# Tying every weight split behind the evacuation of the last item

## The chip, the cores and the metric

The kernel runs on one core of a Trainium2 chip. The metric is the device time of one execution in microseconds (us). An engine is named by its short form: PE is TensorE, DVE is VectorE, ACT is ScalarE, POOL is GpSimd, SP is SyncE, which here issues loads. Each engine works through its own list of instructions in order, and an instruction whose inputs are not ready holds up all that stand behind it on that engine.

## The reference

One layer of a decoder trunk on a sequence of 512 tokens of width 1024. Three causal mixers are fed from one projection, merged by gates, and followed by a squared-ReLU MLP with a gated per-layer embedding:

```python
proj = x @ w_in
(da_q, da_k, da_v, sb_q, sb_k, sb_v, dl_q, dl_k, dl_v, gates) = jnp.split(proj, ...)
o_da = diff_attention(da_q, da_k, da_v, lam, da_norm, ...)   # 4 heads, two softmax maps each
o_sb = stick_breaking_attention(sb_q, sb_k, sb_v)            # 8 heads
o_dl = dilated_attention(dl_q, dl_k, dl_v, ...)              # 3 groups x 4 heads
g = jax.nn.sigmoid(gates)
merged = g0 * (o_da @ w_branch_da) + g1 * (o_sb @ w_branch_sb) + g2 * (o_dl @ w_branch_dil)
x = layer_norm(ALPHA * x + merged @ w_out)
hid = jax.nn.relu(x @ w_up)
c = jnp.square(hid) @ w_down
ple = jax.nn.sigmoid(x @ w_ple_gate) * (p @ w_ple)
x = layer_norm(ALPHA * x + c + ple)
```

## The kernel before

**Items and splits.** All large products are cut into items (the list `items`). An item is a run of matmuls into one bank of PSUM (`mm`), with the function that copies or adds the finished bank out (`ev`, the evacuation). Weights come in blocks of 128 x 1024. SP loads a block into one of five `raw` buffers, or POOL and SP first sum two blocks (`total`). Each block is then split in two parts that the matmuls need: ACT rounds `raw` to `wh` (L255), and DVE subtracts, `wl = raw - wh` (L258). Each product then takes three matmuls: high by high, high by low, low by high (L84 to L86, for example). `wh` and `wl` live in a ring of seven buffers, so a split can run only when PE has read the block of seven splits ago for the last time; a `raw` buffer comes free when the `wl` made from it is done.

**The loop.** For each item n the loop at the end of the kernel (L1607) makes sure that the blocks that the item needs are split, evacuates the item before it (L1617), issues one to three further splits ahead of need (`pump`, L1619), lets one step of the attention heads run beside it, and writes the item's matmuls. Plain items use two banks in turn, so an evacuation has the time of one item before PE needs the bank again; a product that an attention head reads has no such time.

**Order.** The kernel is written through a scheduling layer that may move an instruction ahead of others on its engine by priority. `tc.issue_after(i)` gives one order that it must keep: what is issued inside stands behind `i` on the same engine. It adds no semaphore. `issue_split` (L233) issues each split behind the instructions in the list `tie`. Only the first stick-breaking head fills that list (L1309), and it is emptied at n = 8 (L1621); from there on splits are not tied to anything but their buffers and data.

**Stages.** In the order of time, with the places that the prediction speaks of:

- to about 470 us: the projections, with the heads between them. A dilated head makes two rows of logits L0 and L12 (L1450, L1466, from `dl_k` and `dl_q`; `dl_k` is evacuated at L322), a normaliser over its three groups (L1484 to L1513, with two small matmuls L1491 and L1493), scales its rows (L1515, L1519), transposes them (L1531, L1540; copies `pt0`, `pt12`), and multiplies with `dl_v` (L1552, L1557). A differential head evacuates `da_k` (L122 to L129), makes logits (L135, L136), a softmax difference `lg` (L1394) and transposes it (L1399).
- 470 to 690 us: gates, branches and `w_out`. Gate products are made by a recursive scheme with cut copies (`cut`, L460 to L477).
- 690 to 735 us: the gates of the embedding in the same scheme (L451 to L466; its operand sums are L733 to L768), and the embedding itself, eight items of six matmuls (L794 to L796, copied to `ple`).
- 735 to 1020 us: the MLP (L881 to L883 and L968 to L970).
- from 1028 us: the last items (L1011 to L1013, L1021 to L1023), token tile by token tile, each followed by its normalisation (L1030, L656 to L668; for the last tile L1042 to L1066).

Of the kernel before, what the change touches and what calls it, by code (L numbers as in the profile page):

```python
# [52 lines left out]
def trunk(tc, a, out):  # L53
    nc = tc.nc
    es = ExitStack()
    with es:
# [85 lines left out]
        st = {"dma": 0, "split": 0}  # L142
# [37 lines left out]
        def add(only=False):  # L180
            if copies and (only or moved[0] < moved[1] + LEAD):
                moved[0] += 1
                t, s = copies.popleft()
                wide = [x.rearrange("(a b) m -> a (b m)", b=4) for x in (t[:, :], s)]
                with tc.issue_after(st["load"]):
                    nc.sync.dma_start(*wide)
            elif sums and not only:
                moved[1] += 1
                t, s = sums.popleft()
                i = nc.gpsimd.dma_start(t, s, accum_op=OP.add, max_dma_last_dim=2048)  # L190
                tc.add_manual_dep(getattr(i, "ins", i), casts[0].name, mybir.DependencyInfo(
                    mybir.DependencyClass.Sync, mybir.DependencyReason.DATA), reason="one sum at a time")
# [38 lines left out]
        tie = []  # L231
# [31 lines left out]
        def pump(limit, most=2):  # L263
            n = 0
            while n < most and st["split"] < len(chunks) and st["split"] < limit + RING:
                fill()
                issue_split()
                n += 1
            fill()
# [357 lines left out]
        def ln_consts(g, b):  # L627
            for n in (g, b):
                t = [slot(n) for _ in range(2)]
                for h in range(2):  # L630
                    src = a[n]
                    nc.sync.dma_start(t[h], bass.AP(tensor=src.tensor, offset=src.offset + 512 * h,
                                                      ap=[[0, P], [1, 512]]))
                lnc[n] = t
# [566 lines left out]
        def tables():  # L1201
            nonlocal tab_g0, tab_g1, tab_g2
            yield from rel_vec(slice(0, 4), [(oh[0][:33, :], 0, 512), (oh[1][:33, 0:128], 512, 128)])
            yield from rel_vec(slice(4, 8), [(oh[1][:33, 128:512], 0, 384)])
            yield from rel_vec(slice(8, 12), [(oh[2][:33, 0:256], 0, 256)])
            yield from rel_vec(slice(12, 16), [(oh[2][:33, 256:512], 0, 256)])
            tab_g0 = shifted(4, 4, 256)
            tab_g1 = shifted(8, 4, 128)
            tab_g2 = shifted(12, 4, 128)

        def turn_tables():
            nonlocal tab_g0, tab_g1, tab_g2
            tab_g0, tab_g1, tab_g2 = [turned(*t) for t in (tab_g0, tab_g1, tab_g2)]

        def da_tables():
            nonlocal tab_da
            tab_da = shifted(0, 4, 512)

        def turn_da():
            nonlocal tab_da  # L1220
            tab_da = turned(*tab_da)
# [10 lines left out]
        def load_consts():  # L1232
            for i in range(3):
                oh.append(slot("oh"))
                nc.sync.dma_start(oh[i][:33, :], a["onehot"][:, 512 * i:512 * i + 512])
            lamt = slot("lamt")[:, :256].rearrange("p (a b) -> p a b", a=4)
            src = a["da_lambda"]
            nc.sync.dma_start(lamt, bass.AP(tensor=src.tensor, offset=src.offset, ap=[[0, P], [64, 4], [1, 64]]))
            lams.append(lamt)
            nc.sync.dma_start(rel[0:32, :], a["rel"])  # L1240
            nc.sync.dma_start(gcol, a["da_norm"])
            nc.sync.dma_start(fold, a["perm"][:, 0:P])
            nc.sync.dma_start(foldT, a["perm"][:, P:2 * P])
            nc.sync.dma_start(exf, a["exf"][:, 0:8])
            nc.sync.dma_start(pick, a["exf"][:, 8:72])

        def make_lam():
            lamt = lams[0]
            lp = one.tile([P, 2], F32, name="lp")
            for i in range(2):  # L1250
                nc.vector.scalar_tensor_tensor(lamt[:, 2 * i, :], lamt[:, 2 * i, :], 1.0, lamt[:, 2 * i + 1, :],
                                               op0=OP.mult, op1=OP.mult, accum_out=lp[:, i:i + 1])
            nc.scalar.activation(lp, lp, AF.Exp)
            nc.vector.tensor_sub(lam, lp[:, 0:1], lp[:, 1:2])
            nc.vector.tensor_scalar(lam, lam, LAM_INIT, -1.0, op0=OP.add, op1=OP.mult)
            nc.vector.tensor_scalar(gcol, gcol, 1.0 - LAM_INIT, None, op0=OP.mult)
# [3 lines left out]
        def load_pT():  # L1260
            for k in range(2):
                pTs[k] = slot("pT")
                nc.sync.dma_start(pTs[k], a["pT"][:, k, :])

        def split_pT():
            for k in range(2):
                raw, h, lo = pTs[k], slot("pTh", F32R), slot("pTl", F32R)
                nc.scalar.copy(h, raw)
                nc.vector.tensor_sub(lo, raw, h.bitcast(F32))
                pTs[k] = (h, lo)  # L1270
# [311 lines left out]
        def step():  # L1582
            clock[0] += 1
            if waiting and sum(e[0] for e in active) + waiting[0][0] <= BANKS and clock[0] - last[0] >= gap[0] \
                    and not (len(waiting) == 20 and active):
                active.append(waiting.popleft() + (clock[0],))
                last[0] = clock[0]
                if len(waiting) <= 20:
                    gap[0] = 1
            for e in list(active):  # L1590
                if (clock[0] - e[3]) % e[2]:
                    continue
                try:
                    next(e[1])
                except StopIteration:
                    active.remove(e)
            for g in list(pending):
                try:
                    next(g)
                except StopIteration:  # L1600
                    pending.remove(g)

        DA_TABS = 41
        due = [0]
        freed = 8
        prev = None
        for n, it in enumerate(items):  # L1607
            if n == first_branch:
                while active or waiting:
                    step()  # L1610
            for f in at.get(n, ()):
                f()
            need = it["need"] or it["c"]
            while any("h" not in c for c in need):
                pump(freed, 1)
            if prev is not None:
                prev[0]["ev"](prev[1])  # L1617

            pump(freed, {1: 3, 3: 0, 4: 0}.get(n, 1 if n < 10 or st["split"] - freed > 3 else 2))  # L1619
            if n == 8:  # L1620
                tie.clear()  # L1621
            if n == 4:
                with tc.issue_after(st["load"]):
                    load_consts()
            if n == 10:
                with tc.issue_after(st["low"]):
                    make_lam()
            if n == 13:
                pending.append(tables())
            if n == 22:  # L1630
                turn_tables()
            if n == DA_TABS:
                da_tables()
            if n == DA_TABS + 4:
                turn_da()
            if n >= 7 and not wout_at + 5 <= n < wout_at + 20 and not gates_at - 2 <= n < gates_at + 2:
                due[0] += it["size"]
                rate = 2.4 if n < 23 else 3 if n < gates_at else 5 if n < gates_at + 14 else 3.5 if n < first_branch else 3 if n < wout_at else 5.5
                while due[0] >= rate:
                    due[0] -= rate  # L1640
                    add(n < 23)
            if n == first_branch + 3:
                load_pT()
            if n == first_branch + 14:
                split_pT()
            if n == wout_at - 6:
                ln_consts("ln1_g", "ln1_b")
                for tt in range(4):
                    load_xn(tt)
            if n == drain[0] - 12:  # L1650
                ln_consts("ln2_g", "ln2_b")
            for f in job_runner:
                f(extra.get(n, 0))
            if n > 1:
                step()
            ps = it["bank"]() if it["bank"] else mm_bank()
            for _ in it["mm"](ps) or ():
                step()
            freed += len(it["c"])
            pump(freed, 0)  # L1660
            prev = (it, ps)
# [98 lines left out]
```

## Time and profile before

| | us |
|---|---|
| median of three runs | 1068.28 (1067.71, 1068.28, 1070.68) |
| the profiled execution | 1068.38 |
| its span, from the first to the last instruction | 1066.7 |
| PE busy | 1044.9 |
| DVE busy | 773.1 |
| ACT busy | 557.6 |
| splits on ACT, L255, 245 of 1.050 each | 255.0 |
| splits on DVE, L258, 245 of 1.221 each | 296.6 |

The rows in the prediction come from the profile of this one execution. A row of the timeline gives the start, the duration, the engine, the line of the code and the tiles (out <- in, numbers left out), and in brackets how long the engine had been idle and what ended that. A matmul's duration overlaps that of the next, so what a wait costs PE is read from starts. Views of waits put a wait down to the instruction that ended it.

### The profile page before, as it was taken

How to read it: one execution, taken by the hardware profiler on the slowest of the kernel's cores; microseconds unless marked ns; L12 is line 12 of the kernel's file. 1: busy time of each engine (PE TensorE's matmuls, PEld its weight loads, DVE VectorE, ACT ScalarE, POOL GpSimd, SP SyncE). 2: the span in 40 equal slices, each digit the busy share in tenths (PEclk: the TensorE clock that was granted, in tenths of full speed). 3: DMA queues.
4: the chain of work that ended last, by engine and by line, in shares of the span. 5: the costliest groups of instructions: out<-in, count | busy, mean ns of one | idle time of the engine just before them, and what ended most of it. 6: DMA issues, size and time to landing. Idle time of an engine off the chain costs nothing.

```text
span 1066.7 us, 14724 instructions
## 1 busy us (share of the span) xinstructions
PE 1044.9 (98%) x5503; PEld 896.6 (84%) x5503; DVE 773.1 (72%) x1328; ACT 557.6 (52%) x908; POOL 86.1 (8%) x107
## 2 busy tenths in 40 slices
PE   8999999999999889999999999999999999999996
PEld 6877788989888678878888888878989989989985
DVE  6888566565444577877767766898888788788786
ACT  6566443434333345777626323366767557557551
POOL 0000101001111000001100100100001101100000
PEclk9999999999999999999999999999999999999998
DMA  7556536339888653175968986247878978976712
GB/s 266 168 214 227 173 137 174 91 87 262 256 238 221 193 176 122 62 214 159 287 186 263 308 278 183 95 147 228 266 228 222 273 188 222 277 184 200 234 58 80
DMA packets 64140, 209.12 MB, mean 196 GB/s; under 512 B 7501, under 2 KB 10461, under 8 KB 62916
## 3 DMA queue, kind: packets, MB, share of 16 engines
q1 hardware_dynamic: 43108, 167.38, 43.3%
q0 software_dynamic: 20384, 39.88, 21.8%
q8 instruction: 43, 0.70, 0.2%
q10 hardware_dynamic: 576, 0.92, 0.2%
q14 instruction: 29, 0.24, 0.1%
HBM read 206.03 MB, written 77.62 MB: 266 GB/s over the span
## 4 chain that ended last, share of the span: by engine, by line
PE 91%; DVE 4%; ACT 3%; DMA 1%; issue 1%; POOL 0%; DVEq 0%; SPq 0%
PE mm L84 6%; PE mm L85 6%; PE mm L86 6%; PE mm L883 5%; PE mm L882 5%; PE mm L881 5%; PE mm L363 3%; PE mm L364 3%; PE mm L365 3%; PE at L451 3%; PE at L454 3%; PE at L453 3%; PE mm L968 2%; PE mm L970 2%; PE mm L969 2%; PE mm L598 2%
## 5 line engine op out<-in xcount | busy, mean ns | idle before, releaser
L258 DVE TENSOR_TENSOR wl<-raw,wh 128x1024 fp32r<-128x1024 f32 x245 | 296.6, 1221 | 118.1 <-ACT wh L255 115.9
L255 ACT CAST wh<-raw 128x1024 fp32r<-128x1024 f32 x245 | 255.0, 1050 | 233.6 <-PE mm L600 33.2
L84 PE MATMUL mm<-xhT,wh 128*128 128x512 f32 x304 | 121.0, 398 | 0.4 <-DVE sb_v L376 0.3
L86 PE MATMUL mm<-xhT,wl 128*128 128x512 f32 x304 | 119.3, 392 | 0.1
L85 PE MATMUL mm<-xlT,wh 128*128 128x512 f32 x304 | 119.3, 392 | 0.0
L883 PE MATMUL mm<-XH,wl 128*128 128x256 f32 x256 | 72.4, 283 | 0.0
L882 PE MATMUL mm<-XL,wh 128*128 128x256 f32 x256 | 72.4, 283 | 0.0
L881 PE MATMUL mm<-XH,wh 128*128 128x256 f32 x256 | 72.4, 283 | 0.0
L84 PEld LDWEIGHTS mm<-xhT,wh 128*128 128x128 f32 x304 | 57.2, 188 | 14.5 <-issue 2.7
L86 PEld LDWEIGHTS mm<-xhT,wl 128*128 128x128 f32 x304 | 57.1, 188 | 12.4 <-DVE wl L258 0.5
L85 PEld LDWEIGHTS mm<-xlT,wh 128*128 128x128 f32 x304 | 57.2, 188 | 10.9
L363 PE MATMUL mm<-wh,xhT 128*128 128x512 f32 x160 | 64.0, 402 | 0.0
L364 PE MATMUL mm<-wl,xhT 128*128 128x512 f32 x160 | 63.3, 396 | 0.0
L365 PE MATMUL mm<-wh,xlT 128*128 128x512 f32 x160 | 63.0, 394 | 0.0
L881 PE MATMUL mm<-xs,wh 128*128 128x256 f32 x192 | 54.3, 283 | 0.0
L882 PE MATMUL mm<-xs,wh 128*128 128x256 f32 x192 | 54.3, 283 | 0.0
L883 PE MATMUL mm<-xs,wl 128*128 128x256 f32 x192 | 54.3, 283 | 0.0
L882 PEld LDWEIGHTS mm<-XL,wh 128*128 128x128 f32 x256 | 49.1, 192 | 0.3
L881 PEld LDWEIGHTS mm<-XH,wh 128*128 128x128 f32 x256 | 49.1, 192 | 0.3
L883 PEld LDWEIGHTS mm<-XH,wl 128*128 128x128 f32 x256 | 49.1, 192 | 0.0
L190 POOL DMA_DIRECT2D total<-total x26 | 23.0, 898 | 298.7 <-ACT wh L255 231.5
L365 PEld LDWEIGHTS mm<-wh,xlT 128*128 128x128 f32 x160 | 38.0, 238 | 3.9
(421 smaller groups left out, 2557.6 us busy)
## 6 DMA issues: line engine op xcount, KB each, us to landing
raw<-total SPq DMA_DIRECT2D x72, 512.0 KB, 5.5
raw<-in_wt_dram SPq DMA_DIRECT2D x38, 512.0 KB, 6.5
total<-in_wu_dram SPq DMA_DIRECT2D x26, 512.0 KB, 7.5
total<-total POOLq DMA_DIRECT2D x26, 512.0 KB, 8.0
raw<-in_wd_dram SPq DMA_DIRECT2D x25, 512.0 KB, 6.6
raw<-in_wu_dram SPq DMA_DIRECT2D x24, 512.0 KB, 5.0
total<-in_wd_dram SPq DMA_DIRECT2D x22, 512.0 KB, 6.9
raw<-in_wv_dram SPq DMA_DIRECT2D x20, 512.0 KB, 3.8
```

Source lines behind the costliest of these rows:

```text
L84: nc.tensor.matmul(ps, wh, xh, start=start, stop=False, skip_group_check=True)
L85: nc.tensor.matmul(ps, wh, xl, start=False, stop=False, skip_group_check=True)
L86: nc.tensor.matmul(ps, wl, xh, start=False, stop=stop, skip_group_check=True)
L255: i = nc.vector.tensor_copy(h, raw) if c.get("dve") else nc.scalar.copy(h, raw)
L258: i = nc.vector.tensor_sub(lo, raw, h.bitcast(F32))
L363: nc.tensor.matmul(ps, x1, c["h"][:, s], start=k == 0, stop=False)
L364: nc.tensor.matmul(ps, x1, c["l"][:, s], start=False, stop=False)
L365: nc.tensor.matmul(ps, x2, c["h"][:, s], start=False, stop=k == 7)
L451: nc.tensor.matmul(ps, h, c["h"][:, s], start=k == 0 and begins, stop=False, skip_group_check=True)
L881: nc.tensor.matmul(o, c["h"][:, s], h, start=first, stop=False, skip_group_check=True)
L882: nc.tensor.matmul(o, c["h"][:, s], lo, start=False, stop=False, skip_group_check=True)
L883: nc.tensor.matmul(o, c["l"][:, s], h, start=False, stop=last, skip_group_check=True)
```

## The change

After each evacuation the loop looks at the instructions that it issued and puts the last one on ACT's queue and the last one on DVE's into `tie`. All splits that follow are issued behind these two, until the next evacuation replaces them. This begins after n = 10.

```diff
         DA_TABS = 41
+        queues = (st["cast"].engine, st["low"].engine)
         due = [0]
...
             if prev is not None:
+                traced = tc.nc.cur_bb.bb.instructions
+                since = len(traced)
                 prev[0]["ev"](prev[1])
+                if n > 10:
+                    tie[:] = {i.engine: i for i in traced[since:] if i.engine in queues}.values()
 
             pump(freed, {1: 3, 3: 0, 4: 0}.get(n, 1 if n < 10 or st["split"] - freed > 3 else 2))
```

An evacuation on one engine alone ties only that engine's half of a split; where it has none, `tie` is emptied. No instruction is added or taken away; their order changes on PE, DVE, ACT and SP.

The first place is ACT at 365 to 378 us, in the normaliser of a dilated head and the evacuation of `da_k` of a differential head (`da_ka`, `da_kb`). Before:

```order
L113 ACTIVATE da_qb_799_3276<-mm_791_3220 64x512
L255 CAST wh_865_3552<-raw_776_3160 128x1024
L1508 ACTIVATE ex_807_3299<-ex_807_3299 128x16
L93 COPY pt0_810_3334<-at_809_3329 128x512
L255 CAST wh_878_3609<-raw_782_3196 128x1024
L122 ACTIVATE da_ka_814_3356<-mm_808_3316 64x512
L123 ACTIVATE da_kb_815_3357<-mm_808_3316 64x512
L126 CAST da_ka_814_3356<-da_ka_814_3356 64x512
L128 CAST da_kb_815_3357<-da_kb_815_3357 64x512
```

Of the change, the same engine and place:

```order
L113 ACTIVATE da_qb_799_3276<-mm_791_3220 64x512
L255 CAST wh_800_3281<-raw_751_3020 128x1024
L1508 ACTIVATE ex_807_3299<-ex_807_3299 128x16
L93 COPY pt0_810_3334<-at_809_3329 128x512
L122 ACTIVATE da_ka_814_3356<-mm_808_3316 64x512
L123 ACTIVATE da_kb_815_3357<-mm_808_3316 64x512
L126 CAST da_ka_814_3356<-da_ka_814_3356 64x512
L128 CAST da_kb_815_3357<-da_kb_815_3357 64x512
L255 CAST wh_818_3368<-raw_762_3083 128x1024
L93 COPY pt12_822_3380<-at_821_3375 128x512
```

The split between the copies and the evacuation of `da_k` is gone from there: the cast behind `da_kb` is now that of `wh_818`, two blocks earlier than `wh_865`, so splits run closer to their use. At 355 us the copy of `dl_k` moves the same way ahead of a `wl` on DVE.

The second place is DVE at 701 to 708 us, in the gates of the embedding. `cut` at L466 reads a finished product and frees its bank; the `wl` are for gate items; `xr`, `xs`, `xt` and `XL` are sums and low parts of the gates' operands. Before:

```order
L258 TENSOR_TENSOR wl_1443_6262<-raw_1383_5995,wh_1442_6261 128x1024
L734 TENSOR_TENSOR xs_1399_6049<-xr_1407_6069,xs_1397_6047 128x2x128
L466 TENSOR_TENSOR cut_1436_6226<-cut_1436_6226,mm_1450_6289 128x512
L258 TENSOR_TENSOR wl_1452_6305<-raw_1390_6039,wh_1451_6304 128x1024
L734 TENSOR_TENSOR xs_1400_6050<-xr_1407_6069,xs_1398_6048 128x2x128
L258 TENSOR_TENSOR wl_1456_6338<-raw_1423_6171,wh_1455_6337 128x1024
L734 TENSOR_TENSOR xs_1403_6053<-xr_1408_6071,xs_1401_6051 128x2x128
L258 TENSOR_TENSOR wl_1461_6353<-raw_1426_6177,wh_1460_6352 128x1024
L734 TENSOR_TENSOR xs_1404_6054<-xr_1408_6071,xs_1402_6052 128x2x128
L258 TENSOR_TENSOR wl_1466_6368<-raw_1439_6232,wh_1465_6367 128x1024
```

Of the change, the same place:

```order
L466 TENSOR_TENSOR cut_1436_6226<-cut_1436_6226,mm_1450_6289 128x512
L734 TENSOR_TENSOR xs_1403_6053<-xr_1408_6071,xs_1401_6051 128x2x128
L734 TENSOR_TENSOR xs_1404_6054<-xr_1408_6071,xs_1402_6052 128x2x128
L466 TENSOR_TENSOR cut_1441_6259<-cut_1441_6259,mm_1454_6322 128x512
L258 TENSOR_TENSOR wl_1443_6262<-raw_1383_5995,wh_1442_6261 128x1024
L760 TENSOR_TENSOR xt_1448_6279<-at_1445_6267,xr_1447_6277 128x512
L258 TENSOR_TENSOR wl_1452_6305<-raw_1390_6039,wh_1451_6304 128x1024
L761 TENSOR_TENSOR xt_1449_6280<-xt_1448_6279,xr_1415_6125 128x512
```

Before, four `wl` followed on the first `cut` and stood ahead of the second, which came 13 rows behind the last row shown; now both `cut` stand ahead of all of them. On PE the two embedding items (L794) that take the freed banks follow each other at once, ahead of the gate item that reads `wl_1443`.

The third place is PE at 1030 us, in the last items. `mm_2057` and `mm_2059` are the two halves of token tile 0, `at_2078` the first half of tile 3, and `at_2079` and `at_2080` the two quarters of its second half. Before, the matmul that first reads `wl_2052` stood two places behind the one with `wh_2051`:

```order
L1023 MATMUL mm_2057_9738<-wh_2039_9656,hl_2037_9644 128x512
L1021 MATMUL mm_2057_9738<-wh_2051_9708,hh_2042_9668 128x512
L1011 MATMUL mm_2059_9759<-wh_2030_9624,hh_2012_9486 128x512
L1022 MATMUL mm_2057_9738<-wl_2052_9709,hh_2042_9668 128x512
L1023 MATMUL mm_2057_9738<-wh_2051_9708,hl_2043_9669 128x512
```

Of the change, the twelve matmuls that now end in it:

```order
L1022 MATMUL at_2078_9899<-wl_2040_9657,hh_2048_9694 128x512
L1023 MATMUL at_2078_9899<-wh_2039_9656,hl_2049_9695 128x512
L1021 MATMUL at_2078_9899<-wh_2051_9708,hh_2053_9721 128x512
L1021 MATMUL at_2079_9924<-wh_2046_9690,hh_2048_9694 128x256
L1022 MATMUL at_2079_9924<-wl_2047_9691,hh_2048_9694 128x256
L1023 MATMUL at_2079_9924<-wh_2046_9690,hl_2049_9695 128x256
L1021 MATMUL at_2079_9924<-wh_2055_9731,hh_2053_9721 128x256
L1021 MATMUL at_2080_9939<-wh_2046_9690,hh_2048_9694 128x256
L1022 MATMUL at_2080_9939<-wl_2047_9691,hh_2048_9694 128x256
L1023 MATMUL at_2080_9939<-wh_2046_9690,hl_2049_9695 128x256
L1021 MATMUL at_2080_9939<-wh_2055_9731,hh_2053_9721 128x256
L1022 MATMUL mm_2057_9738<-wl_2052_9709,hh_2042_9668 128x512
```

`wl_2052` stands four rows later on DVE, behind four sums (L985 to L989), and PE's list has matmuls of tile 3 ahead of it: ten of `at_2078` (three more follow a little later) where four came before tile 2 was done, four of `at_2079` and four of `at_2080` where none did.

## The prediction

> **What bounds the kernel now.** I read the page's head first, then the table of stages, then the timeline wherever TensorE (PE) waits.
>
> ```profile
> span 1066.7 us, 14724 instructions
> PE 1044.9 (98%) x5503; PEld 896.6 (84%) x5503; DVE 773.1 (72%) x1328; ACT 557.6 (52%) x908; POOL 86.1 (8%) x107
> PE 91%; DVE 4%; ACT 3%; DMA 1%; issue 1%; POOL 0%; DVEq 0%; SPq 0%
> ```
>
> PE holds 98% of the span and 91% of the chain that ended last. The change adds and removes no instruction, so only two things can move the time: the gaps between matmuls, and the stretch at the end where PE has finished. The table of stages (columns: stretch, its length, busy PE, PEld, DVE, ACT, POOL, granted clock, DMA share, GB/s) tells where gaps are.
>
> ```profile
> 355.00:392.00 37.00, 30.29 (x150) 24.43 (x149) 24.75 (x88) 17.38 (x44) 1.78 (x2) 0.95 0.51 151
> 690.00:735.00 45.00, 43.70 (x194) 35.23 (x194) 40.52 (x63) 30.06 (x50) 2.24 (x2) 1.00 0.56 182
> 735.00:1020.00 285.00, 285.00 (x1891) 263.59 (x1890) 236.04 (x279) 182.09 (x245) 23.80 (x27) 1.00 0.81 229
> ```
>
> From 735 to 1020 PE never stops; 690 to 735 has small gaps, with VectorE (DVE) at 90%; 355 to 392 is the hole, with no engine near full. The timeline of that hole (start, duration, engine, line, tiles; in brackets the idle time before it):
>
> ```profile
> 355.40 0.39 PE L86 MATMUL mm<-xhT,wl 128*128 128x512 f32 x1
> 355.60 1.04 ACT L255 CAST wh<-raw 128x1024 fp32r<-128x1024 f32 x1 [6.83 <-PE mm L85]
> 356.68 1.23 DVE L258 TENSOR_TENSOR wl<-raw,wh 128x1024 fp32r<-128x1024 f32 x1 [6.64 <-ACT wh L255]
> 357.82 0.68 DVE L322 COPY dl_k<-mm 128x512 f32<-128x512 f32 x1
> 358.56 1.16 PE L1466 MATMUL at<-dl_k,dl_q 128*128 128x128 f32 x8 [2.77 <-DVE dl_k L322]
> 360.94 0.40 PE L84 MATMUL mm<-xhT,wh 128*128 128x512 f32 x1
> 362.32 0.41 PE L1491 MATMUL at<-r,fold 128*128 128x32 f32 x2 [0.99 <-DVE r L1484]
> ...
> 374.27 0.39 PE L86 MATMUL mm<-xhT,wl 128*128 128x512 f32 x1
> 374.51 1.04 ACT L255 CAST wh<-raw 128x1024 fp32r<-128x1024 f32 x1 [2.77 <-DMA raw<-in_wga_dram]
> 377.23 0.39 PE L135 MATMUL at<-da_ka,da_qa 128*128 128x256 f32 x1 [2.57 <-ACT da_ka L126]
> 377.87 0.50 PE L135 MATMUL at<-da_kb,da_qb 128*128 128x256 f32 x1 [0.25 <-ACT da_kb L128]
> 381.95 1.95 PE L1557 MATMUL at<-pt,dl_v 128*128 128x128 f32 x16
> ```
>
> The cast at 355.60 needs a ring buffer that PE has just stopped reading, so ScalarE (ACT) idled 6.83 us. DVE sat behind it in its own queue, and the copy dl_k, whose product had long been finished, came third. PE, at an attention matmul that needs dl_k, waited for all of it. At 374.5 the same happens on ACT, there because the weights of a far later block landed late: da_ka stands behind that cast. No weight was missing either time; an early split stood ahead of a late evacuation.
>
> **Part 1: the hole, the gain.** Busy time cannot price it, since matmuls overlap; I count starts. A 512-column matmul follows the last after 0.23 us and a 256-column one after 0.12 us:
>
> ```profile
> 1052.07 0.39 PE L1023 MATMUL mm<-wh,hl 128*128 128x512 f32 x1
> 1052.30 0.39 PE L1012 MATMUL at<-wl,hh 128*128 128x512 f32 x1
> ...
> 1058.11 0.28 PE L1022 MATMUL at<-wl,hh 128*128 128x256 f32 x1
> 1058.23 0.28 PE L1023 MATMUL at<-wh,hl 128*128 128x256 f32 x1
> ```
>
> From 355.40 to 358.56 PE loses 3.16 - 0.23 = 2.93; from 360.94 to 362.32, 1.15 (r is late because dl_k was); from 374.27 to 377.23, 2.73; then 0.52; and from 377.87 to 381.95 fifteen 256-column matmuls take 4.08 instead of 1.80, which is 2.28. Together 9.6 us. A part of the last term is the clock:
>
> ```profile
> 359.00:360.00 1.00, 1.00 (x9) 0.94 (x8) 1.00 (x10) 0.00 (x0) 0.00 (x0) 1.00 0.88 316
> 378.00:379.00 1.00, 1.00 (x4) 0.97 (x5) 0.94 (x3) 0.43 (x1) 0.00 (x0) 0.50 1.08 348
> 382.00:383.00 1.00, 1.00 (x12) 1.00 (x11) 1.00 (x8) 0.17 (x1) 0.00 (x0) 1.00 0.36 97
> ```
>
> From 378 the granted clock is 0.50, and by 382 it is back; after the first, as long, it stayed 1.00 (359). [...] The trace shows the halving right behind the second wait, and I count it as going; the other reading is among the rivals.
>
> In the new order dl_k is copied when its product ends and da_ka stands ahead of the split, so these waits go. Next late is the normaliser of this head. Its matmul L1493 stands five projection matmuls later than before, so 16 of them, not 21, cover the chain from it to the transposes L1531:
>
> ```profile
> 364.92 0.30 PE L1493 MATMUL at<-r,foldT 128*128 128x32 f32 x2
> 367.81 1.23 DVE L258 TENSOR_TENSOR wl<-raw,wh 128x1024 fp32r<-128x1024 f32 x1
> 369.86 1.07 DVE L1515 TENSOR_SCALAR L<-L,mxx 128x128 f32<-128x128 f32 x4
> ```
>
> The first half of L1515 is done at about 370.4, 5.5 us after L1493; one split (367.81) lies inside, and one does in the new order too. Cover is 16 x 0.23 + 0.14 = 3.8, so PE waits 1.7. Gain: 9.6 - 1.7 = **7.9 us**; from 5.5 (the clock loss stays, or the pt copies on ACT and DVE, now behind a split, are late by a bit) to 9.6 (no new wait).
>
> **Part 2: one differential head at 455, a small gain.**
>
> ```profile
> 455.83 0.39 PE L453 MATMUL mm<-wl,xhT 128*128 128x512 f32 x1
> 456.62 0.61 DVE L1394 SCALAR_TENSOR_TENSOR lg<-lg,rr,lg 128x384 f32<-128x384 f32 x1
> 457.29 0.55 PE L1399 MATMUL at<-ident,lg 128*128 128x128 f32 x3 [1.08 <-DVE lg L1394]
> ```
>
> The wait is 1.46 - 0.23 = 1.23, behind a split of 1.23 us that now comes after lg. About 0.3 stays, since lg itself takes 0.61: gain **0.9** (0 to 1.2). At about 579 two gate splits move behind a cut copy and come late by part of their 1.23 us: loss **0.5** (0 to 1.2).
>
> **Part 3: the gates after the first normalisation, a loss.** Here DVE is the near bound (40.52 of 45), so later splits are not free.
>
> ```profile
> 701.90 0.39 PE L451 MATMUL at<-wh,XH 128*128 128x512 f32 x1
> 702.37 0.68 DVE L466 TENSOR_TENSOR cut<-cut,mm 128x512 f32<-128x512 f32 x1
> 709.90 0.50 PE L451 MATMUL at<-wh,XH 128*128 128x512 f32 x1 [1.02 <-ACT XH L733]
> ```
>
> Each L466 frees one of two product banks. Before, PE does seven gate matmuls ahead of the first item of L794 and nineteen between it and the second, while the L466 come. In the new order both items of L794 follow at once, each needs a bank, and the splits of the gate items stand behind both L466 (the second moves up 17 rows). PE is there at 701.9. The first L466, done at 703.05 before, has one more split of 1.23 ahead: done about 704.4, wait 2.5. PE then uses six matmuls, 1.4, and the second L466, behind two more short adds, ends 0.3 after that. The wl of the gate item that follows comes right behind it, 1.2 later, and PE has few matmuls left that can do without: wait 0.8. Two more splits, now behind some ten adds of 0.3 to 0.7, cost about 0.6 each. Sum 4.8, against gaps of 2.0 in this stretch now (1.17 of it at 709.90): loss **2.8**, from 0 (DVE catches up) to 4.2 (three splits waited for in full, 3 x 1.23 + 2.5 - 2.0).
>
> **Part 4: the tail, a loss.** After the last matmul of token tile 2 (1052.07) PE has 3.2 us of 512-column and 2.9 us of 256-column matmuls of tile 3 left, which hide a part of tile 2's normalisation.
>
> ```profile
> 1052.50 0.69 DVE L1030 SCALAR_TENSOR_TENSOR xn<-xn,mm 128x512 f32<-128x512 f32 x1 [0.51 <-PE mm L1023]
> 1056.77 1.41 DVE L668 SCALAR_TENSOR_TENSOR xn<-xn,lr,ln_b 128x512 f32<-128x512 f32 x2
> ```
>
> The end is this DVE and ACT chain, 14.4 us from 1052.30 to the end of the span. In the new order the wl of one of the last blocks stands four rows later on DVE, and PE's list pulls 9 more 512-column and 8 256-column matmuls of tile 3 ahead of it. PE's total is unchanged, so tile 2 ends 9 x 0.23 + 8 x 0.12 = 3.0 later and the chain with it. Back come about 0.9: the first add of tile 3 (L1042) and its statistics fit into DVE's waits for ACT now. Loss **2.1**, from 1.0 (more fits in) to 3.2.
>
> **What costs nothing.** From 735 to 1020 splits come some 5 us later.
>
> ```profile
> 1018.53 1.23 DVE L258 TENSOR_TENSOR wl<-raw,wh 128x1024 fp32r<-128x1024 f32 x1 [1.66 <-ACT wh L255]
> 1034.85 0.39 PE L1012 MATMUL at<-wl,hh 128*128 128x512 f32 x1
> ```
>
> This split is first read 15 us after it ends; by the new order no block between 735 and 1020 comes under about 7. From 60 to 350 the lead is longer. SP's loads wait for the same splits (a raw buffer comes free with the wl) and slip with them; the ring of raw blocks keeps five ahead. POOL's list does not move. If that cover were gone, PE would wait at each block.
>
> **The sum**, against the profiled execution (1068.38, of which 1066.7 span and 1.7 around it): -7.9 - 0.9 + 0.5 + 2.8 + 2.1 = -3.4, **1065.0**. The median of the runs is 1068.28, 0.1 lower, and is what a measurement is held against; 0.3% (3.2 us) is about what one can tell from no change, so faster begins at 1065.1. The forecast stands on that edge.
>
> **Rivals.**
> - Losses without their price: the gates and the tail have slack that a hand count does not see, and parts 3 and 4 cost 1 together. 1068.38 - 7.9 - 0.9 + 0.5 + 1 = 1061.1. For it: 4.5 us of DVE idle in the gate stretch. Against: DVE's order there is fixed.
> - A new wait takes the place of the old: the same head's normaliser and its copies are late by all they could be, 5.5 gain at most half kept (4), losses as above: 1068.4 - 4 - 0.9 + 5.4 = 1068.9, no change. For it: the chain of the head runs in one line over PE, DVE and ACT.
> - The slow stretch at 378 is not the wait's doing and stays, up to 2.3: 1065.0 + 2.3 = 1067.3. For it: the first wait is longer and has none. Against: the other rows of the table stand at 1.00. [...]
> - The other side: DVE becomes the bound of the long stage 735 to 1020. An evacuation waits for the item's last matmul, and the splits behind it now wait too. DVE has 285 - 236 = 49 us to spare; if the added idle passes that and the 7 us of lead, each further us is PE's. An excess of 7, a seventh of that spare, gives 1072. Against: a lead of 7 after 5 of delay.
> - The order does nothing, because ring buffers decide when a split runs: 1068.4. Against: at 374.5 a load decided, and evacuations do change place.
>
> **How the numbers follow.** Forecast 0.46 (its own range 1062.5 to 1067.5), cheap losses 0.20, new wait 0.18, slow stretch 0.05, DVE-bound 0.08, nothing 0.03. Half of the forecast and all of the cheap case are faster: 0.43; slower (over 1071.5): 0.08; the rest, within 0.3%: 0.49. The range takes in the cheap case and the new wait: 1061 to 1070.
>
> **What would show it.** Right: dl_k at 348 instead of 357.8, no wait over 1 us at L1466 and L135, a granted clock of 1.00 from 378 to 382, PE waiting some 1.7 at L1531 for L; waits of PE at L794 for L466; the last L1023 of tile 2 some 3 us, not 6, before PE's end. Wrong: gaps between 735 and 1020, or waits of PE for wl.

## The result and the profile after

| | before | after |
|---|---|---|
| median, us | 1067.85 (1066.67 to 1070.68, 10 runs) | 1065.35 (1064.81 to 1066.84, 10 runs) |
| ratio | | 0.9975 [0.9965, 0.9985] |
| the profiled execution, us | 1068.38 | 1066.84 |
| its span, us | 1066.7 | 1065.1 |

The change makes the kernel faster by 0.25%, with an interval from 0.15% to 0.35%. The forecast was 1065.0. The profiled execution of after is the slowest of its ten, 1.5 us over the median, so its span shows only 1.6 of the 2.5 us.

The head of the page after:

```profile
span 1065.1 us, 14646 instructions
PE 1044.5 (98%) x5503; PEld 896.0 (84%) x5503; DVE 770.4 (72%) x1328; ACT 552.8 (52%) x908; POOL 85.8 (8%) x107
PE 89%; DVE 4%; issue 3%; ACT 1%; DMA 1%; POOL 0%; DVEq 0%; SPq 0%; ACTq 0%; POOLq 0%
```

Each engine has as many instructions as before, and its busy time is that of before within 1% (ACT's is 4.8 us less); the total is 78 lower by instructions that only wait, branch or issue. "Issue" in the chain rises from 1 to 3%. What moved shows only in the stages (stretch, length, busy PE, PEld, DVE, ACT, POOL, granted clock, DMA share, GB/s):

```profile
345.00:382.00 37.00, 35.72 (x189) 29.77 (x188) 22.52 (x81) 15.93 (x41) 2.10 (x3) 1.00 0.62 171
...
680.00:730.00 50.00, 47.70 (x210) 38.60 (x209) 43.49 (x66) 31.16 (x54) 1.91 (x2) 0.97 0.44 140
730.00:1012.00 282.00, 282.00 (x1867) 260.55 (x1866) 228.79 (x273) 175.33 (x238) 23.77 (x27) 1.00 0.81 231
```

The hole is nearly filled (35.72 of 37, where 30.29 of 37 stood), the long stage is still without a gap, and the gates of the embedding have lost both PE time and clock. The hole in the timeline of after:

```profile
348.09 0.69 DVE L322 COPY dl_k<-mm 128x512 f32<-128x512 f32 x1 [2.65 <-PE mm L86]
...
355.58 0.39 PE L86 MATMUL mm<-xhT,wl 128*128 128x512 f32 x1
355.81 1.05 PE L1466 MATMUL at<-dl_k,dl_q 128*128 128x128 f32 x8
362.31 0.23 DVE L1497 TENSOR_TENSOR sel<-at,pick 128x64 f32<-128x64 f32 x1 [1.27 <-PE at L1493]
364.10 0.47 PE L84 MATMUL mm<-xhT,wh 128*128 128x512 f32 x1 [1.28 <-DVE da_qb L105]
367.47 0.70 PE L1531 MATMUL at<-ident,L 128*128 128x128 f32 x3
371.78 0.28 PE L135 MATMUL at<-da_ka,da_qa 128*128 128x256 f32 x1
```

`dl_k` is copied at 348.09 instead of 357.82, and the logits (L1466) and those of the differential head (L135) follow the matmul ahead of them without idle time. The one wait left is new: at 364.10 PE needs a bank that `da_qb`'s evacuation on DVE (L105) has yet to free, and DVE had itself stood idle for 1.27 us at `sel` (L1497), for PE's L1493.

The gates, first the timeline:

```profile
682.13 0.69 DVE L700 SCALAR_TENSOR_TENSOR xn<-xn,mm 128x512 f32<-128x512 f32 x1 [1.84 <-PE mm L694]
685.13 2.35 DVE L258 TENSOR_TENSOR wl<-raw,wh 128x1024 fp32r<-128x1024 f32 x2
695.24 0.40 PE L454 MATMUL mm<-wh,XL 128*128 128x512 f32 x1
696.85 0.69 DVE L466 TENSOR_TENSOR cut<-cut,mm 128x512 f32<-128x512 f32 x1
697.59 0.50 PE L794 MATMUL mm<-wh,pTh 128*128 128x512 f32 x1 [1.95 <-DVE cut L466]
```

and the stages of 1 us behind the wait:

```profile
697.00:698.00 1.00, 0.41 (x2) 0.37 (x3) 1.00 (x3) 1.00 (x3) 0.00 (x0) 1.00 0.50 197
698.00:699.00 1.00, 1.00 (x5) 0.76 (x4) 0.49 (x2) 1.00 (x3) 0.00 (x0) 0.62 0.00 0
699.00:700.00 1.00, 1.00 (x4) 0.76 (x3) 0.74 (x2) 1.00 (x2) 0.00 (x0) 0.50 0.00 0
700.00:701.00 1.00, 1.00 (x3) 0.78 (x3) 1.00 (x2) 1.00 (x3) 0.00 (x0) 0.50 0.00 0
701.00:702.00 1.00, 1.00 (x4) 0.78 (x3) 1.00 (x2) 1.00 (x3) 0.00 (x0) 0.67 0.21 33
```

PE waits 697.59 - 695.24 - 0.23 = 2.12 at the first item of L794, and right behind it the granted clock is at half, which costs seven matmuls 0.2 each. Last, the tail:

```profile
1050.85 0.39 PE L1023 MATMUL mm<-wh,hl 128*128 128x512 f32 x1
1051.27 0.69 DVE L1030 SCALAR_TENSOR_TENSOR xn<-xn,mm 128x512 f32<-128x512 f32 x1 [0.51 <-PE mm L1023]
1054.00 0.28 PE L1023 MATMUL at<-wh,hl 128*128 128x256 f32 x1
1060.18 1.53 DVE L1066 SCALAR_TENSOR_TENSOR xn<-xn,lr,ln_b 128x512 f32<-128x512 f32 x3
```

PE's last matmul starts at 1054.00, where it was 1058.23: the gain up to there is 4.2 us. From there to the end of the span it was 8.5 us and is now 11.1.

Place by place, counted as the prediction counts (starts beyond 0.23 us for 512 columns and 0.12 for 256; the tail from PE's last start to the end of the span):

| place | before | after | change | predicted |
|---|---|---|---|---|
| 345 to 392, the hole | 9.6 | 1.8 | -7.8 | -7.9 |
| 392 to 470, a differential head | 1.2 | 0.7 | -0.5 | -0.9 |
| 470 to 680 | 0 | 1.2 | +1.2 | +0.5 |
| 680 to 735, the gates | 2.0 | 4.2 | +2.2 | +2.8 |
| 735 to 1015 | 0 | 0 | 0 | 0 |
| tail | 8.5 | 11.1 | +2.6 | +2.1 |
| sum | | | -2.3 | -3.4 |

The spans of the two profiled executions, from which the table is taken, differ by 1.6 only: the table leaves out late starts of less than 0.15 us, and with them the hole gives -7.6, the head -0.3, the stretch from 470 to 680 +1.5 and the gates +2.0, together with the tail -1.8. The medians differ by 2.5. One profile alone is a blunt measure here, since executions differ where no item is tied: ahead of 20 us the gaps are 1.7 to 3.9 us in the fourteen profiles of this document, above all one wait for the first casts (L344), 2.35 us in the change and 0.2 in e2.

### The profile page after: what moved, and what is told of

It is laid out like the page before. It is cut to its first block, busy times and chain, and to the rows that moved or that the text cites. A ratio compares the mean times of both kernels' runs of the same rounds, so it can differ in the third digit from the quotient of the medians.

```text
span 1065.1 us, 14646 instructions
## 1 busy us (share of the span) xinstructions
PE 1044.5 (98%) x5503; PEld 896.0 (84%) x5503; DVE 770.4 (72%) x1328; ACT 552.8 (52%) x908; POOL 85.8 (8%) x107
## 4 chain that ended last, share of the span: by engine, by line
PE 89%; DVE 4%; issue 3%; ACT 1%; DMA 1%; POOL 0%; DVEq 0%; SPq 0%; ACTq 0%; POOLq 0%
PE mm L84 6%; PE mm L86 6%; PE mm L85 6%; PE mm L883 5%; PE mm L882 5%; PE mm L881 5%; PE mm L363 4%; PE mm L364 3%; PE mm L365 3%; PE at L451 2%; PE at L454 2%; PE at L453 2%; PE mm L968 2%; PE mm L969 2%; PE mm L970 2%
## 5 line engine op out<-in xcount | busy, mean ns | idle before, releaser
L84 PE MATMUL mm<-xhT,wh 128*128 128x512 f32 x304 | 121.3, 399 | 1.5 <-DVE da_qb L105 1.3
L84 PEld LDWEIGHTS mm<-xhT,wh 128*128 128x128 f32 x304 | 57.2, 188 | 15.6 <-issue 4.3
L85 PEld LDWEIGHTS mm<-xlT,wh 128*128 128x128 f32 x304 | 57.2, 188 | 10.8
```

Source lines behind the costliest of these rows:

```text
L84: nc.tensor.matmul(ps, wh, xh, start=start, stop=False, skip_group_check=True)
L85: nc.tensor.matmul(ps, wh, xl, start=False, stop=False, skip_group_check=True)
```

## The experiments

The theory (A in the expectations) is the prediction's: four places with ties of their own, one large gain and three losses, which can be had apart. Rivals stand in each expectation. Each experiment changes at which items, or on which engine, `tie` is filled, and e6 the place of one more instruction; at the items left out `tie` is emptied, which is the order of before. Of each edit the main lines are shown. `n` counts the items of the loop: the evacuation of `dl_k` is item 46's, the hole lies at items 45 to 58, the gates of the embedding and the embedding at 129 to 150, the last items at 295 to 311. Every kernel was timed beside the kernel before on the same chip; the median of before was 1068.09 to 1068.66 there, so the ratios are compared.

| run | tied | median, us | before there | ratio |
|---|---|---|---|---|
| e1 | items 11 to 284 | 1063.61 (1061.81 to 1064.24) | 1068.66 | 0.9946 [0.9928, 0.9964] |
| e2 | the hole | 1061.41 (1060.75 to 1061.73) | 1068.66 | 0.9926 [0.9909, 0.9943] |
| e3 | all but the hole | 1073.67 (1073.05 to 1075.67) | 1068.66 | 1.0047 [1.0031, 1.0063] |
| e4 | as e1, without the gates | 1061.01 (1060.36 to 1063.02) | 1068.66 | 0.9930 [0.9909, 0.9950] |
| e5 | items 45 to 75 | 1061.64 (1061.22 to 1061.79) | 1068.09 | 0.9941 [0.9929, 0.9954] |
| e6 | as e5, `sel` behind the evacuation | 1061.00 (1060.45 to 1061.26) | 1068.09 | 0.9935 [0.9922, 0.9949] |
| e7 | the hole, DVE alone | 1070.71 (1068.87 to 1071.40) | 1068.09 | 1.0023 [1.0014, 1.0032] |
| e8 | the hole, ACT alone | 1060.61 (1059.66 to 1060.75) | 1068.09 | 0.9930 [0.9918, 0.9942] |
| e9 | all, ACT alone | 1061.90 (1061.14 to 1063.32) | 1068.66 | 0.9941 [0.9928, 0.9953] |
| e10 | items 45 to 68, ACT alone | 1060.54 (1059.78 to 1060.60) | 1068.66 | 0.9926 [0.9912, 0.9940] |
| e11 | items 11 to 284, ACT alone | 1059.64 (1059.31 to 1060.26) | 1068.38 | 0.9921 [0.9907, 0.9935] |
| e12 | as e11, DVE too at the gates | 1061.82 (1061.45 to 1061.96) | 1068.38 | 0.9939 [0.9925, 0.9953] |

### Which place is worth what: e1 to e4

**e1, the last items untied.**

```diff
-                if n > 10:
+                if 10 < n < 285:
                     tie[:] = {i.engine: i for i in traced[since:] if i.engine in queues}.values()
+                elif n > 10:
+                    tie.clear()
```

> The ties of the change, but none for the last 27 items (from item 285 on), so that TensorE's list at the end is that of before: nothing of token tile 3 but four matmuls is pulled ahead of tile 2. Theory A (the tail loss is the order of the last items): from the last matmul's start to the end of the span 8.5 us as before instead of 11.1, time 1065.35 - 2.6 = 1062.7. Rival B (the tail is late because splits were late all through the MLP stage, whatever the last items do): no better than 1065.3. The wait at L794 near 695 and the hole stay as with the change.

By the ratios e1 is 0.0029 x 1068 = 3.1 us below the change. In its profile (span 1060.1):

```profile
696.14 0.50 PE L794 MATMUL mm<-wh,pTh 128*128 128x512 f32 x1 [1.95 <-DVE cut L466]
...
696.95 0.40 PE L794 MATMUL mm<-wh,pTh 128*128 128x512 f32 x1
...
1051.65 0.28 PE L1023 MATMUL at<-wh,hl 128*128 128x256 f32 x1
```

From PE's last start to the end are 1060.1 - 1051.65 = 8.45 us, as before the change: the tail's 2.6 us come from the ties of the last items. The wait at L794 is there as in the change, but this time no half clock follows: the granted clock is 1.00 from 695 to 705, and L795, L796 and the next L794 start 0.23 to 0.34 apart. What makes the difference was not shown.

**e2, the hole alone.**

```diff
+                if 44 < n < 59:
```

> Ties only for items 45 to 58, the stretch of the hole at 355 to 392 us; no tie before and after. Theory A (the gain is these two late evacuations and nothing else): waits of TensorE in 345 to 392 fall from 9.6 to about 1.8 as with the change, the rest is as before, time 1067.85 - 7.8 = 1060.0. Rival B (the gain needs the ties around, or losses elsewhere belong to having the waits gone, such as loads that now collide): 1063 to 1066.

The gaps at 345 to 392 are 1.8, as in the change; from 392 to 470 they are 1.9 and from 680 to 735 2.0, close to before. The gain is 7.25 by the medians and 7.9 by the ratio. So fourteen items carry all of the change's gain, and more: the ties elsewhere take back two thirds of it.

**e3, all but the hole.**

```diff
+                if 10 < n and not 44 < n < 59:
```

> The ties of the change everywhere but at items 45 to 58. Theory A: the hole is back, 7.8 us, the losses stay: 1065.35 + 7.8 = 1073.1. Rival B: the ties ahead of it already keep the ring short, the splits come late there too, and part of the gain stays: 1066 to 1070.

In its profile the hole is back, 9.45 us of gaps, with the same wait for `dl_k`:

```profile
357.77 1.16 PE L1466 MATMUL at<-dl_k,dl_q 128*128 128x128 f32 x8 [2.77 <-DVE dl_k L322]
```

The time is 5.0 above before. That is what the ties outside the hole cost by themselves, against 5.5 in the table of places (-0.5 + 1.2 + 2.2 + 2.6).

**e4, the gates untied as well.**

```diff
+                if 10 < n < 285 and not 127 < n < 148:
```

> As the first of these, and also no ties at items 128 to 147, the gates of the embedding. Theory A (the wait at the first L794 and the half clock behind it come from the splits moved behind both L466): the gaps between 680 and 735 fall from 4.2 to 2.0, 2.2 us below the first of these, 1060.5. Rival B (the clock drop there is not the wait's doing): only 0.8 below it, 1061.9, with a stretch of granted clock 0.5 still near 698.

By the medians it is 2.6 below e1, though the intervals overlap. The gaps from 680 to 735 are 1.9, as before, against 3.4 in e1's profile; neither has a half clock there. So the gates' loss goes with the ties of items 128 to 147; e11 and e12, whose ranges lie apart, give its size again.

### Can what is left at the heads be had: e5 and e6

**e5, the hole and the head after it.**

```diff
+                if 44 < n < 76:
```

> Ties for items 45 to 75, the hole and the heads up to 470 us. With ties for the hole alone, TensorE still waited 1.14 and 0.72 us for lg at L1399 near 443 and 452. Theory A (those are splits ahead of lg, as in the hole): they fall to about 0.4 each, 1.1 us less than with ties for the hole alone, ratio to before about 0.9915. Rival B (lg is late by its own chain): no difference, ratio 0.9926.

The waits at L1399 fall to 0.35 and 0.40. But 1.3 us of new waits come at 516, 610 and 615, in the branches; the two at L598 in its profile:

```profile
611.02 0.47 PE L598 MATMUL mm<-wh,oTh 128*128 128x512 f32 x1 [0.38 <-ACT oTh L93]
...
615.71 0.50 PE L598 MATMUL mm<-wh,oTh 128*128 128x512 f32 x1 [0.33 <-DVE cut L604]
```

Nothing is gained over the hole alone. I put these waits down to splits that the ties of items 69 to 75 delay, which e10 tests.

**e6, the wait that is left in the hole.** The multiplication `sel` is what DVE stands idle at, ahead of the evacuation that PE needs. Here it is issued behind the evacuation, too:

```diff
+            with ExitStack() as behind:
+                for i in tie:
+                    if i.engine == st["low"].engine:
+                        behind.enter_context(tc.issue_after(i))
-            nc.vector.tensor_mul(sel, px[:, 0:64], pick)
+                nc.vector.tensor_mul(sel, px[:, 0:64], pick)
```

> As the one before, and the head's operation sel (L1497) is tied on VectorE behind the last evacuation too. What is left of the hole with the change is 1.45 us near 362 at the first matmul of an item (L84), which waits for its bank; the evacuation that frees it (L105) stands behind sel, and sel waits 1.27 us for TensorE's L1493. Theory A (the bank is late because sel holds up the evacuation): the 1.45 goes, the transposes L1531 wait some 0.4 for the normaliser, which now stands behind a split: 1.2 us less than the one before. Rival B (the bank is late because the copies on ScalarE are late): the 1.45 stays, no difference.

```profile
362.39 0.47 PE L84 MATMUL mm<-xhT,wh 128*128 128x512 f32 x1 [0.19 <-DVE da_qb L105]
```

This row is the rest of the wait, 0.36 instead of 1.45 counted by starts, and the gaps of the hole are 1.0 instead of 1.8. So the cause of the wait is shown: the order of `sel` and L105. Against e5 the medians gain 0.6, half of what was expected; their ratios' intervals overlap.

### Which engine's tie does it: e7 to e10

**e7, the hole with the tie on DVE alone.** `queues[1:]` is DVE, `queues[:1]` ACT.

```diff
+                if 44 < n < 59:
+                    tie[:] = {i.engine: i for i in traced[since:] if i.engine in queues[1:]}.values()
```

> Ties for items 45 to 58 on VectorE alone; the casts on ScalarE are free to run early as before. Theory A (the first wait, dl_k, is on VectorE, and the second, da_ka, on ScalarE): dl_k is in time, L1466 does not wait (4.1 us with what follows it); a cast that waits for a ring buffer or a load still stands ahead of da_ka, and L135 waits 2 to 3 us: between before and ties on both, about 1068.66 - 4.3 = 1064.4. Rival B (it is the subtraction on VectorE that delays both): as with ties on both, 1061.4.

It is slower than before, which neither theory expected. In its profile:

```profile
357.01 1.04 ACT L255 CAST wh<-raw 128x1024 fp32r<-128x1024 f32 x1 [6.83 <-PE mm L85]
...
373.02 1.04 ACT L255 CAST wh<-raw 128x1024 fp32r<-128x1024 f32 x1 [2.58 <-PE mm L85]
375.73 0.38 PE L135 MATMUL at<-da_ka,da_qa 128*128 128x256 f32 x1 [2.57 <-ACT da_ka L126]
...
460.83 0.55 PE L1399 MATMUL at<-ident,lg 128*128 128x128 f32 x3 [1.76 <-DVE lg L1394]
```

The casts still stand idle on ACT (6.83 and 2.58 us); `dl_k` on DVE is free of them, `da_ka` on ACT is not. So in the hole theory A holds: the gaps there are 6.5 instead of 9.6. But from 392 to 470 they are 4.6 instead of 1.2, with new waits at 401 to 403 (1.55 and 0.77) and at 459 to 461 (1.93), outside the tied items, where DVE's order has changed as a consequence: at 454.86 and 456.07 two subtractions stand in the middle of a softmax. Before has one there (451.83) and one right ahead of `lg` (455.49), and DVE waits for POOL in both (0.86 and 0.91), so how the order makes the wait longer is open, and why the scheduling layer comes to it, too. Gain and loss by place cancel; of the 2.4 us by which the profiled span is longer than before's, 1.1 lies ahead of 20 us, where no item is tied. How much of the median's 2.6 is of that kind is not known.

**e8, the hole with the tie on ACT alone.**

```diff
+                if 44 < n < 59:
+                    tie[:] = {i.engine: i for i in traced[since:] if i.engine in queues[:1]}.values()
```

> Ties for items 45 to 58 on ScalarE alone. Theory A (a subtraction cannot run before its cast, so a late cast moves it too): both waits go, as with ties on both, 1061.4. Rival B (VectorE needs its own tie): the wait at L1466 stays, about 1065.

This one tie does all: the gaps of the hole are 1.1, less than with both, I take it because a `wl` follows its cast anyway and DVE is not held beyond that. The wait at L84 is 0.32 in its profile:

```profile
363.19 0.47 PE L84 MATMUL mm<-xhT,wh 128*128 128x512 f32 x1 [0.16 <-DVE da_qb L105]
```

**e9, ACT alone, at all items.**

```diff
                 if n > 10:
+                    tie[:] = {i.engine: i for i in traced[since:] if i.engine in queues[:1]}.values()
```

> The change with ties on ScalarE alone, at all items from 10 on. Theory A (a subtraction follows its cast, so ScalarE's ties do nearly all, gains and losses): the hole's waits go, TensorE waits about 2 at the first L794, and at the end nine more matmuls of tile 3 stand ahead of tile 2: as the change, ratio to before 0.9975, about 1065.4. Rival B (the losses in the gates and the tail are VectorE's ties): 1061 to 1062.

It is 0.0034 x 1068 = 3.6 us below the change: that is what DVE's ties cost. The gates have gaps of 1.5 instead of 4.2. DVE at the gates, in its profile:

```profile
677.26 2.35 DVE L258 TENSOR_TENSOR wl<-raw,wh 128x1024 fp32r<-128x1024 f32 x2
679.54 0.68 DVE L700 SCALAR_TENSOR_TENSOR xn<-xn,mm 128x512 f32<-128x512 f32 x1
...
692.29 0.68 DVE L466 TENSOR_TENSOR cut<-cut,mm 128x512 f32<-128x512 f32 x1
```

Two subtractions run while DVE would stand idle at L700 in the change. The tail's loss stays: 10.8 us from PE's last start to the end. That part of it is ACT's tie.

**e10, ACT alone, the hole and the head after it.**

```diff
+                if 44 < n < 69:
+                    tie[:] = {i.engine: i for i in traced[since:] if i.engine in queues[:1]}.values()
```

> Ties on ScalarE alone for items 45 to 68: the hole and the two heads behind it, and nothing of the gate items behind those, where ties up to item 75 cost 1.3 us near 516, 610 and 615. Theory A (gains and losses add by place): the waits of 1.13 and 0.71 at L1399 near 443 and 452 fall to about 0.4 each, none near 610: 1.1 below ties on ScalarE for items 45 to 58 (ratio 0.993), ratio 0.992. Rival B (what is taken from one wait comes back at the next): ratio 0.993 again.

The waits at L1399 are again 0.35 and 0.40, but waits of 0.54 and 0.49 at 609 and 614 come although no item from 69 on is tied. My assignment of e5's new waits to the ties of items 69 to 75 falls. Beside e8 (0.9926 and 0.9930, intervals overlapping) no gain can be told.

### The best version, and what the gates' loss is: e11 and e12

**e11, ACT alone, up to the last items.**

```diff
+                if 10 < n < 285:
+                    tie[:] = {i.engine: i for i in traced[since:] if i.engine in queues[:1]}.values()
```

> Ties on ScalarE alone, from item 10 to 284: the version of ties on ScalarE at all items without the last 27. Theory A (the tail's loss is the order of the last items and adds to the rest): TensorE's last matmul to the end 8.5 us instead of 10.8, 2.3 us below ties on ScalarE at all items (ratio 0.9941), ratio 0.992, faster than the change and than before. Rival B (what is won at the tail is lost to a later end of TensorE): ratio 0.994.

This has the lowest ratio of the kernels here, 0.9921 [0.9907, 0.9935] against before, and is by the ratios 5.8 us below the change; but its interval overlaps those of all runs above other than e3 and e7. Its tail is 8.4 again. Its gates:

```profile
677.93 2.35 DVE L258 TENSOR_TENSOR wl<-raw,wh 128x1024 fp32r<-128x1024 f32 x2
680.21 0.68 DVE L700 SCALAR_TENSOR_TENSOR xn<-xn,mm 128x512 f32<-128x512 f32 x1
...
693.69 0.50 PE L794 MATMUL mm<-wh,pTh 128*128 128x512 f32 x1 [0.25 <-DVE cut L466]
```

**e12, the same with DVE's tie put back at the gates.**

```diff
+                if 10 < n < 285:
+                    tie[:] = {i.engine: i for i in traced[since:] if i.engine in queues[:1 + (127 < n < 148)]}.values()
```

> As the one before, with ties on VectorE added at items 128 to 147, the gates of the embedding. Theory A (the wait at the first L794 comes from VectorE's ties: two subtractions stand behind L700, which waits 1.84 us for TensorE, and VectorE, busy from there on, is late by that at L466): the wait at L794 is 2.1 instead of 0.4, 1.7 to 3 us above the one before, the upper end if the granted clock halves behind the wait. Rival B (the wait is late for another reason, ties elsewhere on VectorE): no wait over 0.5 there, no difference.

In its profile, the timeline and one stage behind the wait:

```profile
679.87 0.69 DVE L700 SCALAR_TENSOR_TENSOR xn<-xn,mm 128x512 f32<-128x512 f32 x1 [1.84 <-PE mm L694]
695.34 0.50 PE L794 MATMUL mm<-wh,pTh 128*128 128x512 f32 x1 [1.94 <-DVE cut L466]
```

```profile
698.00:699.00 1.00, 1.00 (x4) 0.81 (x3) 1.00 (x2) 1.00 (x2) 0.00 (x0) 0.50 0.00 0
```

All three come back together: DVE's 1.84 us idle at L700, PE's wait of 2.1 at L794, and the half clock; the time rises by 2.2 us. So DVE's tie is the cause at the gates, not ACT's.

## Why the prediction was right

**What bounds, and the sum.** The reading that only gaps and the tail can move held: busy PE is the same to 0.4 us. The sum of the places is 1.1 us above the one predicted, with misses of both signs. That the forecast is only 0.35 us off is in part luck: it took 3.4 from the one profiled execution (1068.38), and the median of before came out at 1067.85, with a gain of 2.5.

**Part 1, the hole.** Right, 7.8 for 7.9, and shown by e2 and e3: with the hole's ties alone the gain is there, without them it is not. One step was wrong in its place. The new wait was to be 1.7 at L1531, for the normaliser; L1531 comes 0.15 late, and the wait of 1.45 is at L84, for a bank. What I had not followed is that DVE, too, has an instruction that waits for PE (`sel`), with an evacuation behind it, the same fault that the change mends for splits. e6 shows this cause. That price and place missed and the size fitted is chance. The last term of the sum was read too large: of the "fifteen 256-column matmuls" behind 377.87 six are of L1552, which start 0.21 to 0.22 apart at full clock too (24 times in the change), and two more have 128 columns, so about 1.8 of its 2.28 were loss; late starts of 0.2 at 349 and 0.3 at 367, which it left out, bring the total back to 9.6.

**Part 1, whose queue.** I named ACT's idle cast first and DVE's queue behind it. e8 against e7 bears out the order of that chain: the tie on ACT alone brings all of the gain, the tie on DVE alone frees `dl_k` but not `da_ka`, and what it gains in the hole (3.1) is lost in the waits behind.

**Part 2.** The term was mis-sized: 0.9 of gain was 0.5, since 0.35 and 0.38 are left of two waits, and the 0.5 of loss behind it was 1.2, in several waits of 0.2 to 0.4 from 493 to 614. One of them, 0.35 at L453 (572.30), is a wait for a `wl`, which the prediction had among its signs of being wrong. In e5 and e10, which tie items 59 to 68 too, 1.0 us of waits stands at 609 to 616; e2 and e8, which don't, have none there. By which split it comes was not settled.

**Part 3, the gates.** The size held, 2.2 for 2.8; the step failed. I had one split ahead of the first L466 (wait 2.5), then small waits behind. The wait is 2.12, but DVE is late for another reason: it stands idle 1.84 us at L700 (682.13), for PE, while two tied `wl` stand behind it (685.13) which e9 and e11 run ahead of it, and it does not catch up until L466 at 696.85. The later waits did not come as priced, and a half clock of 1.4 us took their place; in e1, where the wait is the same and the clock stays full, the loss is 1.4, so that the size held is in part luck. e9 and e11 (no idle time, wait 0.4) and e12 (all back) show it. I counted where the splits stand among DVE's instructions; I did not ask which of them would have filled a wait.

**Part 4, the tail.** Right in mechanism: tile 2's last matmul stands 1054.00 - 1050.85 = 3.15 before PE's last, for 6.2 before the change, as forecast. The loss was 2.6 for 2.1, since of the 0.9 to come back 0.4 did: from L1030 to the end of DVE's last addition (L1066) it was 10.83 (1052.50 to 1063.33) and is 10.44 (1051.27 to 1061.71). e1 shows that the ties of the last items are the cause, and e9 that ACT's alone are enough.

**What costs nothing.** Right: 282.00 of 282 from 730 to 1012. With it the rival of a DVE-bound long stage fell.

**The other rivals.** Losses without their price fell (they cost 4.8 at the gates and the tail). The new wait in place of the old fell: it left at most 4 us of part 1's gain, and 7.8 were kept. The order does change the time (e3, slower by 5.0). The slow stretch at 378 went with its wait: the clock is 1.00 from 345 to 382 after, and at half again in e3 (0.50 at 378, with PE idle from 374 to 376) and e7 (0.50 at 377, behind 2.57 at L135), where that wait is back. But the step behind it, that such a wait brings the half clock, is only half true: in e1 the same wait at L794 as in the change (1.95) had none behind it, and what else it takes was not shown.

## What to carry to other kernels

When an early task stands ahead of a late one in an engine's queue, the first thing to find is which instruction stands idle there, and to tie that one alone: the tie of the cast on ACT carried all of the gain, and the second tie on DVE cost 3.6 us. An order rule is worth what it is worth at each place, so it is tried by place: with both ties, 14 items gave more than 300 did, and the end of a kernel, where nothing is left to hide a delay, is looked at by itself. Before a filler is moved behind an evacuation, ask what will fill the wait that it filled until now.

## What was not expected of the hardware

In these profiles the granted clock of PE fell to half in stretches of nearly one length. Taking twice the missing share of the slices of 1 us, the stretch at 698 in the change is 2 x (0.38 + 0.50 + 0.50 + 0.33) = 3.42 us, that at 378 before is 2 x (0.50 + 0.50 + 0.50 + 0.20) = 3.40, and e12's at 696 is 3.42. The idle time ahead of them was 1.95, 2.57 and 1.94 us, shorter than the stretch itself. Waits as long did not always have one behind them: 2.77 us at 358 before, and 1.95 at 696 in e1, had none.

The traces give the times of the changes. In the change the granted clock fell at 698.24, 0.65 us behind the start of L794 at 697.59, was back at 701.66, and fell again at 1056.64, 2.4 behind PE's end. In before it fell at 377.98, 0.75 behind the start of L135 at 377.23, was back at 381.39, and fell again at 1060.64, 2.1 behind PE's end. What decides whether a wait is followed by such a stretch was not shown. At the gates of the change it cost 1.4 us, seven matmuls at 0.2 each; half of its length, 1.7 us, is my estimate of what one costs at most, and so of its part in the hole's 9.6 before. Whether these two stretches come in every execution was not shown either.

The same stretch gives a scale to the spread between runs. One lowers the mean clock of the span by 1.7 / 1065 = 0.0016. Six runs of the change have a mean clock of 0.997 and take 1065.1 on average, four have 0.994 or 0.995 and take 1066.1. The mean also takes in the half clock at the very end, where PE has no more work. In the profiles of before, the change, e1, e4, e11 and e12 it starts 2.1 to 5.1 us behind PE's end. An estimate from these: if it does so in all ten runs, it lasts, from PE's end at 1054.3 to the end of the span at 1065.1, 5.7 to 8.7 us (8.5 in the profile), so the mean is 0.9959 to 0.9973 without a stretch ahead of it and 0.9943 to 0.9957 with one. By this, four of the ten runs have one and six none, and the 1.0 us between them fits it roughly. That it stands at the gates in all four is not shown, since only one execution was profiled.
